# Grouped attention: the value product with tokens on partitions, division by the softmax sums behind it

## The chip, the cores and the metric

The kernel runs on one core of one Trainium2 chip. The metric is the device time of one execution in microseconds (us); the median over several executions is compared. The engines are named as in the profile: PE (TensorE, matrix products; PEld are its weight loads), DVE (VectorE), ACT (ScalarE), POOL (GpSimd) and SP (SyncE, which issues transfers).

## The reference, cut to what matters

The model is two layers of a hybrid block: a state-space branch, grouped attention, differential attention and a gated recurrence, merged, and then a feed-forward part. 256 latent tokens and 256 context tokens run through it; the second layer gives out the latent tokens alone. The change touches grouped attention only: 8 query heads of 64 features, two key and value heads.

```python
def gqa_core(q, k, v):
    s = jnp.einsum('bqgrd,bkgd->bgrqk', q, k) * ATTN_SCALE
    p = softmax32(s).astype(v.dtype)
    return jnp.einsum('bgrqk,bkgd->bqgrd', p, v)
```

## The kernel before

Activations lie with features on partitions and tokens along the free axis. Layer 0 has four tiles of 128 tokens (two latent ones, which attend to all 512 keys, and two context ones, which attend to 256); layer 1 has the two latent tiles. Dense products are made in three float32r matmuls of high and low parts (`mm3`, lines 267 to 269), into four PSUM accumulators of the pool `big`. Attention uses four others, of the pool `small`.

Grouped attention is made in two halves of four heads (`gqa_half`). Its queries come from `q_half`: for each token tile a dense product into a `big` tile, then the norm and the rotation (`rope_of`: a product with the cosines into `fo`, L611, one with the sines into `fth`, L617, and their sum, L619), four transposes (`twice`, L625) and the split into high and low parts. The accumulator is free only when L611 and L617 have read it. The name `fth` stands for two buffers, which tiles take in turn in program order.

For each token tile and head, `soft` makes the scores of 512 or 256 keys (two matmuls, L731 and L732), the row maximum (L734, DVE), the exponential with its sum (L737, ACT), the reciprocal of the sum (L762) and the scaled exponentials (L763, both DVE). Two steps later, `value` transposes the probabilities in blocks of 128 keys (`pT`: L589 on PE, the copy L742 on ACT) and, once both heads of a pair are there, multiplies them with the values (L777): V is the stationary side with 64 columns, the transposed probabilities move with 128 columns, and the two heads write partitions 0 to 63 and 64 to 127 of the output. After two pairs a copy (L780, DVE) puts the tile into the half's output, which has features on partitions already.

`staged` runs the stages with a lag of two steps and gives their instructions high priority; `along` puts merge products of another branch (L1076 on: a dense product with 512 or 256 columns into `big`) between them in program order. The order on the engines is then set by the scheduler of the framework, which plays the program through with its own times and picks what is ready; so a change in one loop can move instructions elsewhere.

Of the kernel before, what the change touches and what calls it, by code (L numbers as in the profile page):

```python
# [9 lines left out]
F32 = mybir.dt.float32  # L10
# [4 lines left out]
OP = mybir.AluOpType  # L15
# [192 lines left out]
def _build(ctx, nc, tc, I, out, dbg):  # L208
    PSUM = bass.MemoryType.PSUM

    def pool(name, bufs, **kw):
        return ctx.enter_context(tc.tile_pool(name=name, bufs=bufs, **kw))
# [9 lines left out]
    sp = pool("sp", 4)  # L222
# [3 lines left out]
    V, S, G, PE = nc.vector, nc.scalar, nc.gpsimd, nc.tensor  # L226
# [5 lines left out]
    def small(n=512):  # L232
        p = pm.tile([128, 512], F32, name="small")
        return p[:, :n]

    def tt(name, n=512, dt=F32, bufs=None):

        x = tmp.tile([128, 512], dt, name=name, bufs=bufs or 3)
        return x[:, :n]
# [4 lines left out]
    def blk(ap, d):  # L244
        return ap.rearrange("p (h d) -> p h d", d=d)

    def bc(ap, shape):
        return ap.to_broadcast(shape)
# [306 lines left out]
    class Mixer:  # L555
# [198 lines left out]
                yield  # L754

        def gqa_half(self, i, qs, o):
            ets, ops = {}, {}

            def soft(c, _):
                t, pr, half = c  # L760
                e, s, k0, kn = self.probs(qs[t], self.gk, 2 * pr + half, half, t)
                V.reciprocal(s, s)  # L762
                V.tensor_scalar(e, e, s, None, op0=OP.mult)  # L763
                return e, k0, kn

            def value(c, x):
                t, pr, half = c
                e, k0, kn = x
                ets[half] = self.pT(e, kn)
                if not half:  # L770
                    return
                if not pr:
                    ops[t] = small(256)
                for kb in range(kn):
                    for z in range(2):
                        hs = slice(z * 64, z * 64 + 64)
                        PE.matmul(ops[t][hs, pr * 128:(pr + 1) * 128], self.gv[:, k0 + kb, hs],  # L777
                                  ets[z][:, kb * 128:(kb + 1) * 128], start=kb == 0, stop=kb == kn - 1)
                if pr:
                    V.tensor_copy(o[:, :, t * 128:(t + 1) * 128], blk(ops.pop(t), 128))  # L780

            return self.staged([(t, pr, z) for t in range(self.nt) for pr in range(2) for z in range(2)],
                               [soft, value], 2)

        def diff_half(self, i, qs, kT, v, o):
            p, n = self.p, self.n
# [407 lines left out]
    def place(c, ps):  # L1194

        row = ap_.tile([2, 512], F32, name="row", bufs=2)
        V.tensor_copy(row, ps[0:2])
        tp = small(8)
        for i in range(4):
            PE.transpose(tp[:, i * 2:i * 2 + 2], row[:, i * 128:(i + 1) * 128], ident[0:2, 0:2])  # L1200
        i0 = c % 2 * 8 + c // 2 * 4
        V.tensor_copy(mods[0][:, i0:i0 + 4], tp.rearrange("p (i v) -> p i v", v=2))

    before = None
    for c in range(4):

        ps = small()
        for k in range(0, KT, 2):
            z = c * 4 + k // 2
# [17 lines left out]
    for l in range(DEPTH):  # L1227
# [44 lines left out]
        qs = mx.q_half("gq", 0, 0)  # L1272
# [8 lines left out]
        qs = mx.q_half("gq", 0, 1)  # L1281
# [6 lines left out]
        qs = mx.q_half("dq", 2, 0)  # L1288
# [5 lines left out]
        qs = mx.q_half("dq", 2, 1)  # L1294
# [46 lines left out]
```

## Time and profile before

| what | value |
|---|---|
| median of 3 runs | 1808.97 us |
| the profiled execution | 1808.46 us, span 1806.7 us |
| share of the span in which PE is busy | 94% |
| DVE, ACT, POOL | 69%, 51%, 47% |
| mean granted clock of PE | 0.975 of full speed |

The span runs from the first to the last instruction; what is around it, some 1.8 us, is part of the time. PE's clock has two levels, 2.4 GHz (1.00) and 1.2 GHz (0.50); a mean between them is a mixture of both. A PE that is busy isn't at its peak: matmuls overlap, and what one costs is read from one start to the next.

### The profile page before, as it was taken

To read this page: it belongs to the slowest core of one execution; us is meant where nothing else is said; L and a number is where in the kernel's file an instruction comes from. 1 tells how busy PE (TensorE), PEld (TensorE's weight loads), DVE (VectorE), ACT (ScalarE), POOL (GpSimd) and SP (SyncE) were. 2 spreads that over 40 slices of the span, in tenths; PEclk is the share of its full clock that TensorE was granted. 3 is DMA by queue.
4 is the path that set the end of the run, shared out by engine and by line. 5 is a ranking of instruction groups with operands and counts; after the bars stand their busy time and mean duration, and the time that the engine had idled before them with its cause. 6 is when DMAs were issued, how large, how long until landed. Compare 5 with 4: busy or idle time off the path is not lost.

```text
span 1806.7 us, 27888 instructions
## 1 busy us (share of the span) xinstructions
PE 1702.3 (94%) x10734; PEld 1490.2 (82%) x10734; DVE 1243.0 (69%) x2233; ACT 925.0 (51%) x1685; POOL 855.6 (47%) x522
## 2 busy tenths in 40 slices
PE   6979999989989998999999999978999999989999
PEld 1866788878888787987778889866888999989998
DVE  6697757766868676798756465677767667567664
ACT  3635654544544554465544343646555555556554
POOL 4353655342535657566534342454773345433443
PEclk9989999999999999999999999988999999989999
DMA  7221423221323355535655453222243133445553
GB/s 294 87 94 52 139 90 119 89 90 45 105 77 113 98 183 209 187 123 172 201 186 176 136 166 106 87 94 93 95 141 117 48 118 120 172 150 184 187 184 127
DMA packets 52037, 237.10 MB, mean 131 GB/s; under 512 B 9664, under 2 KB 12608, under 8 KB 34496
## 3 DMA queue, kind: packets, MB, share of 16 engines
q1 hardware_dynamic: 28080, 179.46, 28.7%
q10 hardware_dynamic: 23824, 55.86, 9.7%
q8 instruction: 85, 1.39, 0.3%
q14 instruction: 48, 0.39, 0.1%
HBM read 234.18 MB, written 1.11 MB: 130 GB/s over the span
## 4 chain that ended last, share of the span: by engine, by line
PE 39%; DVE 5%; DMA 2%; POOL 2%; ACT 2%; issue 1%; ACTq 0%; POOLq 0%; DVEq 0%; SPq 0%
PE big L267 12%; PE big L268 12%; PE big L269 12%; DMA w<-in_w 1%; POOL whl L251 1%; DMA wa<-in_w 1%; POOL wa L431 1%; PE small L777 1%; ACT whl L256 1%; PE small L589 1%; DVE whl L251 1%; PE small L625 0%; DVE fo L552 0%; PE small L731 0%; DVE B L1033 0%
## 5 line engine op out<-in xcount | busy, mean ns | idle before, releaser
L251 POOL TENSOR_TENSOR whl<-w,whl 128x1024 fp32r<-128x1024 f32 (+3 forms) x194 | 450.6, 2326 | 528.0 <-ACT whl L256 490.2
L267 PE MATMUL big<-hh,whl 128*128 128x256 f32 (+1 forms) x1632 | 549.0, 341 | 24.6 <-ACT sq L668 9.1
L268 PE MATMUL big<-hl,whl 128*128 128x256 f32 (+1 forms) x1632 | 549.5, 338 | 0.8 <-POOL hl L251 0.8
L269 PE MATMUL big<-hh,whl 128*128 128x256 f32 (+1 forms) x1632 | 549.6, 338 | 0.0
L256 ACT CAST whl<-w 128x1024 fp32r<-128x1024 f32 (+3 forms) x342 | 334.6, 985 | 171.3 <-PE big L269 81.9
L267 PEld LDWEIGHTS big<-hh,whl 128*128 128x128 f32 x1632 | 312.2, 193 | 61.0 <-issue 15.7
L268 PEld LDWEIGHTS big<-hl,whl 128*128 128x128 f32 x1632 | 314.3, 193 | 33.3 <-issue 3.4
L269 PEld LDWEIGHTS big<-hh,whl 128*128 128x128 f32 x1632 | 314.4, 193 | 33.2 <-issue 3.4
L251 DVE TENSOR_TENSOR whl<-w,whl 128x1024 fp32r<-128x1024 f32 (+2 forms) x150 | 198.7, 1326 | 68.1 <-ACT whl L256 67.7
L552 DVE SCALAR_TENSOR_TENSOR fo<-big,pp,fo 128x510 f32<-128x510 f32 (+2 forms) x224 | 141.0, 633 | 79.4 <-ACT fo L544 75.8
L431 POOL TENSOR_TENSOR wa<-wa,crow 128x1024 f32<-128x1024 f32 x48 | 126.9, 2646 | 76.4 <-DVE fo L435 44.8
L267 PE MATMUL big<-whl,hl 128*128 128x256 f32 (+1 forms) x512 | 148.9, 292 | 3.5 <-DVE sq L1044 3.0
L268 PE MATMUL big<-whl,hh 128*128 128x256 f32 (+1 forms) x512 | 149.7, 293 | 2.0 <-POOL whl L251 2.0
L269 PE MATMUL big<-whl,hh 128*128 128x256 f32 (+1 forms) x512 | 149.4, 292 | 0.0
L267 PE MATMUL big<-act,whl 128*128 128x256 f32 (+1 forms) x392 | 125.4, 320 | 4.1 <-POOL whl L251 4.1
L269 PE MATMUL big<-act,whl 128*128 128x256 f32 (+1 forms) x392 | 125.6, 321 | 0.0
L268 PE MATMUL big<-act,whl 128*128 128x256 f32 (+1 forms) x392 | 125.4, 320 | 0.0
L544 ACT ACTIVATE fo<-big,pp 128x512 f32<-128x512 f32 (+1 forms) x104 | 71.0, 683 | 97.4 <-PE big L269 89.6
L267 PEld LDWEIGHTS big<-whl,hl 128*128 128x128 f32 x512 | 100.1, 196 | 5.3 <-DVE sq L1044 3.2
L268 PEld LDWEIGHTS big<-whl,hh 128*128 128x128 f32 x512 | 100.5, 196 | 3.7 <-POOL whl L251 2.2
L269 PEld LDWEIGHTS big<-whl,hh 128*128 128x128 f32 x512 | 100.4, 196 | 1.2 <-issue 1.0
L267 PE MATMUL big<-bo,whl 128*128 128x512 f32 (+1 forms) x256 | 89.1, 349 | 9.7 <-POOL whl L251 9.3
(296 smaller groups left out, 3265.3 us busy)
## 6 DMA issues: line engine op xcount, KB each, us to landing
w<-in_w SPq DMA_DIRECT2D x136, 1024.0 KB, 4.9
wa<-in_w ACTq DMA_DIRECT2D x64, 512.0 KB, 3.6
w<-in_w SPq DMA_DIRECT2D x16, 768.0 KB, 4.3
w<-in_w SPq DMA_DIRECT2D x16, 640.0 KB, 3.9
bcm<-in_w ACTq DMA_DIRECT2D x14, 512.0 KB, 3.6
q<-csd ACTq DMA_DIRECT2D x24, 256.0 KB, 4.3
wa<-in_w SPq DMA_DIRECT2D x11, 512.0 KB, 8.5
xm<-in_xT ACTq DMA_DIRECT2D x8, 512.0 KB, 7.5
```

Of the source, the lines that this page charges most:

```text
L251: eng.tensor_tensor(o, v, hi.bitcast(F32), op=OP.subtract)
L256: S.copy(m.h, v)
L267: PE.matmul(ps, a.l, b.h, start=start, stop=False)
L268: PE.matmul(ps, a.h, b.l, start=False, stop=False)
L269: PE.matmul(ps, a.h, b.h, start=False, stop=stop)
L431: G.tensor_tensor(w, w, cr, op=OP.mult)
L544: S.activation(o, ps, AF.Identity, scale=wt[:, nc_ + c:nc_ + c + 1], bias=b[:, c:c + 1])
L552: V.scalar_tensor_tensor(os_, is_, wt[:, j * nc_ + c:j * nc_ + c + 1], os_, op0=OP.mult, op1=OP.add)
L589: PE.transpose(ps[:, i * 128:(i + 1) * 128], s, ident)
L777: PE.matmul(ops[t][hs, pr * 128:(pr + 1) * 128], self.gv[:, k0 + kb, hs], ets[z][:, kb * 128:(kb + 1) * 128], start=kb == 0, stop=kb == kn ...
```

## The change

Each head is now a step of its own in `value`. The transposed probabilities are the stationary side (128 columns), V moves with 64 columns, and the output has tokens on partitions and the four heads of the half side by side along the free axis. The exponentials aren't scaled; the reciprocals of a tile's four sums are kept in `rs4`, and one DVE product per token tile (L780 in the changed kernel) multiplies the four heads' outputs with them on the way out of PSUM, into a buffer of the name `fth`. A third stage, `place`, two steps later, transposes that tile in two blocks (PE, L589 through `transposes`) and copies it into the half's output (ACT, L787).

```diff
             def soft(c, _):
-                t, pr, half = c
-                e, s, k0, kn = self.probs(qs[t], self.gk, 2 * pr + half, half, t)
-                V.reciprocal(s, s)
-                V.tensor_scalar(e, e, s, None, op0=OP.mult)
+                t, hd = c
+                e, s, k0, kn = self.probs(qs[t], self.gk, hd, hd % 2, t)
+                if not hd:
+                    rs[t] = sp.tile([128, 4], F32, name="rs4", bufs=2)
+                V.reciprocal(rs[t][:, hd:hd + 1], s)
                 return e, k0, kn
 
             def value(c, x):
-                t, pr, half = c
+                t, hd = c
                 e, k0, kn = x
-                ets[half] = self.pT(e, kn)
-                if not half:
+                et = self.pT(e, kn)
+                if not hd:
+                    ops[t] = small(256)
+                vs = slice(hd % 2 * 64, hd % 2 * 64 + 64)
+                for kb in range(kn):
+                    PE.matmul(ops[t][:, hd * 64:(hd + 1) * 64], et[:, kb * 128:(kb + 1) * 128],
+                              self.gv[:, k0 + kb, vs], start=kb == 0, stop=kb == kn - 1)
+                if hd < 3:
                     return
-                if not pr:
-                    ops[t] = small(256)
-                for kb in range(kn):
-                    for z in range(2):
-                        hs = slice(z * 64, z * 64 + 64)
-                        PE.matmul(ops[t][hs, pr * 128:(pr + 1) * 128], self.gv[:, k0 + kb, hs],
-                                  ets[z][:, kb * 128:(kb + 1) * 128], start=kb == 0, stop=kb == kn - 1)
-                if pr:
-                    V.tensor_copy(o[:, :, t * 128:(t + 1) * 128], blk(ops.pop(t), 128))
+                f = tt("fth", 256, bufs=2)
+                V.tensor_tensor(blk(f, 64), blk(ops.pop(t), 64), bc(rs.pop(t)[:, :, None], [128, 4, 64]), op=OP.mult)
+                return f
+
+            def place(c, f):
+                t, hd = c
+                if hd == 3:
+                    self.transposes([f[:, 0:128], f[:, 128:256]],
+                                    lambda q: S.copy(o[:, :, t * 128:(t + 1) * 128], q))
```

The order of the instructions moves with it. On DVE, in the first half of layer 0's grouped attention, the rotation of the second half's first query tile (L611, L617, tile `tab`) stood between the early heads before. The names are `sm` the sums, `e` the exponentials, `tab` the table of sines and cosines.

```order
L762 RECIPROCAL sm<-sm 128x1
L611 TENSOR_TENSOR fo<-big,tab_2500 128x256
L617 TENSOR_TENSOR fth<-big,tab_2500 128x256
L302 TENSOR_SCALAR xs<-xs 128x512
L635 TENSOR_SCALAR ss<-ss 128x4
L763 TENSOR_SCALAR e<-e,sm 128x512
```

In the changed kernel L611 of that tile stands at about the same place, but L617 comes only behind the product L780 of the half's last token tile, on the same engine:

```order
L734 TENSOR_REDUCE mx<-small 128x1
L780 TENSOR_TENSOR fth<-small,rs_2907 128x256
L764 RECIPROCAL rs_2987<-sm 128x1
L734 TENSOR_REDUCE mx<-small 128x1
L764 RECIPROCAL rs_2987<-sm 128x1
L780 TENSOR_TENSOR fth<-small,rs_2987 128x256
L617 TENSOR_TENSOR fth<-big,tab_2500 128x256
L619 TENSOR_TENSOR fo<-fo,fth 128x256
```

L617 has moved from the fourth head's place to behind the sixteenth's.

On PE, in the same half, at the heads of the context tiles, merge products of 512 columns (L267 to L269) stood between one head's matmuls and the next before:

```order
L267 MATMUL big<-hh,whl 128x512
L268 MATMUL big<-hl,whl 128x512
L589 MATMUL small<-cst,e 128x128 x3
L731 MATMUL small<-kp,q 128x256
L732 MATMUL small<-kp,q 128x256
L589 MATMUL small<-cst,e 128x128 x3
L777 MATMUL small<-et,gv 64x128
L269 MATMUL big<-hh,whl 128x512
```

The same heads in the changed kernel, where L775 is the value product:

```order
L775 MATMUL small<-gv,et 128x64 x4
L589 MATMUL small<-cst,e 128x128 x4
L731 MATMUL small<-kp,q 128x256
L732 MATMUL small<-kp,q 128x256
L589 MATMUL small<-cst,e 128x128 x4
L731 MATMUL small<-kp,q 128x256
L732 MATMUL small<-kp,q 128x256
L775 MATMUL small<-gv,et 128x64 x4
L589 MATMUL small<-cst,e 128x128 x2
L775 MATMUL small<-gv,et 128x64 x5
```

The merge products have moved behind the half's last transposes; from the last head of 512 keys on, attention stands alone on PE until then.

## Rows read from the trace of the kernel before

**Rows 1.** The page's part 1: busy us, share of the span, instructions.

```profile
PE 1702.3 (94%) x10734; PEld 1490.2 (82%) x10734; DVE 1243.0 (69%) x2233; ACT 925.0 (51%) x1685; POOL 855.6 (47%) x522
```

**Rows 2.** Windows: stretch, us, each engine's busy us, clock, DMA share, GB/s.

```profile
350.00:396.00 46.00, 46.00 (x297) 38.95 (x295) 25.20 (x47) 20.77 (x45) 16.63 (x8) 1.00 0.26 85
396.00:403.40 7.40, 2.13 (x12) 1.25 (x11) 7.40 (x9) 2.65 (x7) 4.84 (x2) 0.84 0.11 44
403.40:410.20 6.80, 6.40 (x46) 4.88 (x45) 5.87 (x12) 4.67 (x11) 2.36 (x1) 0.67 0.66 231
1400.00:1450.00 50.00, 50.00 (x404) 45.61 (x405) 34.01 (x74) 25.49 (x48) 17.68 (x11) 1.00 0.17 57
```

**Rows 3.** Timeline of PE, layer 0: start us, us, engine, line, names, shapes, records.

```profile
324.04 0.28 PE L267 MATMUL big<-whl,hl 128*128 128x256 f32 x1
324.16 0.28 PE L268 MATMUL big<-whl,hh 128*128 128x256 f32 x1
324.37 0.43 PE L777 MATMUL small<-et,gv 128*64 128x128 f32 x2
324.73 0.50 PE L731 MATMUL small<-kp,q 128*128 128x512 f32 x1
325.07 0.39 PE L732 MATMUL small<-kp,q 128*128 128x512 f32 x1
325.30 0.28 PE L269 MATMUL big<-whl,hh 128*128 128x256 f32 x1
...
328.11 0.40 PE L732 MATMUL small<-kp,q 128*128 128x512 f32 x1
328.43 1.09 PE L777 MATMUL small<-et,gv 128*64 128x128 f32 x14
329.45 0.39 PE L269 MATMUL big<-whl,hh 128*128 128x256 f32 x1
329.67 0.28 PE L267 MATMUL big<-whl,hl 128*128 128x256 f32 x1
```

**Rows 4.** Timeline of PE, layer 1: the last block of value products.

```profile
1429.95 1.09 PE L777 MATMUL small<-et,gv 128*64 128x128 f32 x14
```

**Rows 5.** Timeline of PE in `ssd_decay`: 32 and 64 columns over 128 stationary.

```profile
157.90 0.39 PE L846 MATMUL small<-da,cst 128*128 128x32 f32 x2
158.13 0.41 PE L847 MATMUL small<-da,ones 128*128 128x64 f32 x2
158.35 0.47 PE L267 MATMUL big<-hh,whl 128*128 128x512 f32 x1
```

**Rows 6.** Groups by line, DVE: busy us, mean ns, idle us before.

```profile
L763 DVE TENSOR_SCALAR e<-e,sm 128x512 f32<-128x512 f32 (+1 forms) x48 | 30.4, 637 | 1.2
```

**Rows 7.** Timeline of all engines around the gap; in brackets idle before, and releaser.

```profile
396.45 5.14 DVE L763 TENSOR_SCALAR e<-e,sm 128x512 f32<-128x512 f32 x2
396.47 2.34 POOL L431 TENSOR_TENSOR bcm<-bcm,xs 128x1024 f32<-128x1024 f32 x1 [3.88 <-DVE sm L762]
398.78 2.53 POOL L251 TENSOR_TENSOR whl<-w,whl 128x1024 fp32r<-128x1024 f32 x1
399.24 0.63 PE L589 MATMUL small<-cst,e 128*128 128x128 f32 x4 [3.10 <-DVE e L763]
...
402.23 0.69 ACT L737 ACTIVATE e<-small,mx 128x512 f32<-128x512 f32 x1 [4.75 <-DVE mx L734]
...
403.06 1.12 PE L589 MATMUL small<-cst,e 128*128 128x128 f32 x4 [2.16 <-ACT e L737]
```

**Rows 8.** Groups by line and shape, 311 to 445 us: heads of 256 keys.

```profile
L737 ACT ACTIVATE e<-small,mx 128x256 f32<-128x256 f32 x16 | 7.7, 483 | 11.2 <-DVE mx L734 11.2
L734 DVE TENSOR_REDUCE mx<-small 128x1 f32<-128x256 f32 x16 | 6.7, 421 | 12.3 <-PE small L732 12.2
L742 ACT COPY et<-small 128x256 f32<-128x256 f32 x16 | 5.9, 372 | 7.7 <-PE small L589 4.2 <-PE small L777 3.4
```

**Rows 9.** Timeline of DVE: a split of branch 0 beside GpSimd.

```profile
318.28 2.35 DVE L251 TENSOR_TENSOR bo<-xs,bo 128x512 fp32r<-128x512 f32 x1
```

More of the change, by code (lines that the diff above doesn't have):

```diff
@@ L756, in gqa_half @@
         def gqa_half(self, i, qs, o):
-            ets, ops = {}, {}
+            ops, rs = {}, {}
             def soft(c, _):
-                t, pr, half = c
-                e, s, k0, kn = self.probs(qs[t], self.gk, 2 * pr + half, half, t)
-                V.reciprocal(s, s)
-                V.tensor_scalar(e, e, s, None, op0=OP.mult)
+                t, hd = c
[3 more added lines that the diff above has]
+                V.reciprocal(rs[t][:, hd:hd + 1], s)
@@ L779, in value @@
-                if pr:
-                    V.tensor_copy(o[:, :, t * 128:(t + 1) * 128], blk(ops.pop(t), 128))
-            return self.staged([(t, pr, z) for t in range(self.nt) for pr in range(2) for z in range(2)],
-                               [soft, value], 2)
+                et = self.pT(e, kn)
[5 more added lines that the diff above has]
+                              self.gv[:, k0 + kb, vs], start=kb == 0, stop=kb == kn - 1)
@@ new lines, in value @@
+                if hd < 3:
+                    return
+                f = tt("fth", 256, bufs=2)
[6 more added lines that the diff above has]
+                                    lambda q: S.copy(o[:, :, t * 128:(t + 1) * 128], q))
+            return self.staged([(t, hd) for t in range(self.nt) for hd in range(4)], [soft, value, place], 2)
```

## The prediction

> **What bounds the kernel now.** I read the busy times of the page first, then TensorE's (PE's) share in the stretches where grouped attention runs. PE is busy for 1702 of 1807 us, VectorE (DVE), the next one, for 1243 [rows 1]. So a microsecond leaves the run only if it leaves PE's own work or a gap in PE. The loop that the diff rewrites, `gqa_half`, runs from about 311 to 445 us (layer 0, 32 pairs of a head and a token tile) and from 1369 to 1431 us (layer 1, 16). Nearly everywhere in it PE is full: 46.0 of the 46 us up to 396 us, 50.0 of the 50 from 1400 us [rows 2]. Work taken from DVE under that cover is worth nothing by itself; only PE's own instructions count there. One hole lies in the loop: from 396.0 to 403.4 us PE is busy for 2.1 of 7.4 us, and in the 6.8 us after that the mean granted clock is 0.67, so PE runs at 1.2 GHz for a part of them [rows 2]. These two things, PE's own cost and that hole, carry the sum.
>
> **PE's value products.** Before, a value matmul has 64 stationary columns (V) and 128 moving ones; the two heads of a pair write the two halves of the output's partitions. Each float32 matmul is two records in the trace. What a block of them costs is read from one dense neighbour's start to another's [rows 3]: a matmul of 256 columns takes 0.12 us from start to start (324.04 to 324.16), one of 512 columns 0.23 (325.07 to 325.30). A block of 2 records: 324.16 to 325.07 is 0.91 us, less 0.12 and 0.23 for the dense matmul on either side, is 0.56 us. A block of 14: 328.11 to 329.67 is 1.56, less 0.23 and 0.12, is 1.21 us. Twelve records more cost 0.65 us, so two records, one of each head, cost 0.11 together: the two heads overlap fully. What is left is 0.45 us for each block, whatever its length: the entry into that half-array form and the way out. The timeline has 57 blocks, the first at 324.37 us and the last at 1429.95 [rows 3, 4]. So the 320 records cost 160 x 0.11 + 57 x 0.45 = 17.6 + 25.7 = 43.3 us of PE.
>
> After, the transposed probabilities are stationary (128 columns) and V moves with 64 columns, one head at a time: 160 matmuls again, 320 records, in the whole array, with nothing to enter. That form is in the trace of before: the sums of `ssd_decay` move 32 and 64 columns over 128 stationary ones, and four such records move the next start from 157.90 to 158.35 us, 0.112 each [rows 5]. I take 320 x 0.112 = 35.8 us. The bounds are 0.055, half of a pair today, and 0.112; the rows of the very form stand at the upper end. New are 24 transposes of the finished tiles, 48 records, 5.4 us at the same price. On PE that makes 35.8 + 5.4 - 43.3 = -2.1 us.
>
> The Trainium skill, "TensorEngine Tiling (Array Packing)", section "When to Use Tiling", speaks against this edit: for a moving side of 64 columns or fewer it advises to swap the operands and tile the columns in two, which is the form given up here. By that rule alone PE would go from 17.6 to 41.2 us. The 0.45 us of each block is what the rule leaves out; the same page, "Key Properties", says that a change of tiling mode drains the engine, and the trace agrees.
>
> **DVE and ScalarE (ACT).** The 48 scalings of the exponentials go, 30.4 us of DVE, 0.64 in the mean [rows 6]. The 48 reciprocals stay. The 12 copies of the output become 12 products over the same 128x256 elements; I cost the difference at nothing, since PE's full rows cover both, and with that cover gone it would be a few tenths each. ACT gets 12 copies of 256 columns, 0.37 us each by the copies of transposed probabilities [rows 8]: 4.5 us on an engine that is half idle. This matters only where PE starves.
>
> **The hole.** At 396.45 us DVE begins two scalings that take 5.14 us together, in the time in which GpSimd runs two long products (396.47 to 401.31) [rows 7]. PE's transposes wait 3.10 us for the first. The next row maximum is queued behind the second on DVE, its exponential on ACT waits 4.75 us for that, and PE another 2.16 us for the exponential [rows 7]. Gaps: 5.3 us. The clock of 0.67 over 6.8 us in which PE is nearly always busy takes (1 - 0.67) x 6.8 = 2.2 us [rows 2]. Together 7.5 us. After, the transposes read the exponentials straight from ACT, and no scaling stands ahead of a maximum, so I take all 7.5 off. The bounds are 0 and 7.5, since GpSimd's long products stay and other DVE instructions can meet them; that is a rival.
>
> **The new wait.** The finished tile goes into the `fth` buffers, of which there are two, and `rope_of` of the next queries uses the same two. In program order the first two query tiles of the second half get the buffers of the last finished tiles of the first half. The order shows what follows: the rope product L617 of the first query tile stood right behind its partner L611; now it stands behind the last finished tile of the half. Queued behind it on DVE are the rest of that rope and the next tile's. Until it is done, the four query tiles hold all four `big` accumulators, and the merge matmuls of 512 columns, which were spread over the first half, can't start. So PE gets a bare run of attention. By the order, in it are 32 value matmuls (7.2 us at 0.224), 28 transposes of probabilities (6.3), 9 pairs of score matmuls, one with 512 keys (0.46) and 8 with 256 (0.24 each), and 8 transposes of finished tiles (1.8): 17.7 us. Is PE fed in it? ACT has 24 instructions of 0.37 to 0.69 us in it and 9 short readings of sums, some 12 us; DVE has less [rows 7, 8]. In the order a head's transposes come about two heads behind its scores. From scores to exponential it takes some 1.4 us (0.3 to reach DVE, 0.42 maximum, 0.48 exponential, hand-overs), and the heads between cover that. Stepping through the order by hand with these lengths, I find two waits of 0.2 us for a copy and one of 0.8 us at the end, where the last finished tile and then the rope product must pass DVE: 1.2 us. ACT's queue adds to it; I take 3 us. The bounds are 0 and no overlap at all, where a head of 256 keys takes 2.8 us (0.24 + 0.3 + 0.42 + 0.48 + 0.22 + 0.3 + 0.37 + 0.45) in place of 1.0 and one of 512, at 1.6 times that, 4.4 in place of 1.8: 8 x 1.8 + 3 x 2.6 = 22 us. With two heads in flight the rows are near the lower end.
>
> In the second half of layer 0 and in layer 1 the new order leaves dense work between most heads, and layer 1's stretch has no gap today, so there only PE's own sum counts.
>
> **The sum.** The profiled execution took 1808.46 us for a span of 1806.7, and the median shown is 1808.97, so a change of the span goes straight to the median: 1809 - 2.1 - 7.5 + 3 = 1802.4, taken as 1802 us. The scheduler also moves some work of the second layer's recurrence, ahead of its attention; with no row that gives it a sign I allow it 3 us either way. With the other small uncertainties the forecast's own range is 1797 to 1807.
>
> **Rivals.** The hole returns in other clothes: GpSimd's long products still run near the start of the second half, and a DVE instruction of 512 columns that is no scaling took 2.35 us at 318.28 us [rows 9]. For it: those products keep their place in the order. Against it: dense merges now stand between the heads there. Then only PE's own sum is left: 1809 - 2.1 = 1807.
>
> The new wait is dear, and the kernel slower than before: the bare run costs what two heads in flight fail to hide, and the clock falls behind it as it did at 403 us. It decides when it costs more than 9.6 us (2.1 + 7.5). Midway between that and the serial bound of 22 us, 16 us give 1809 - 9.6 + 16 = 1815. For it: 17.7 us without a dense matmul in the order. Against it: the steps above.
>
> The overlap of the two heads was the whole matter: PE pays 41.2 in place of 17.6 us and gets nothing back: 1809 + 23.6 - 7.5 + 3 = 1828. The 0.45 us of each block speaks against it. This is the tiling rule of the Trainium skill taken as it stands.
>
> Narrow matmuls are cheap: at 0.055 us a record PE saves another 18 us: 1784. The rows at 157.90 us speak against it.
>
> **How the numbers follow.** Forecast 0.55 (1802), hole returns 0.17 (1807), dear wait 0.20 (1815), overlap lost 0.03 (1828), cheap records 0.05 (1784). From 1795 to 1813 the range leaves out the cheap records, the lost overlap and half of the dear wait, 0.18. Two per cent, about what a measurement of this kernel can tell from no change, is 36 us, and no case reaches it: within 2% has 0.96, and 0.02 stand on each side for a schedule that goes another way altogether.
>
> **What would show it.** Value records 0.112 us apart, with no step of 0.2 us on the way in or out; no gap of over 1 us on PE where the second half begins, and a clock of 1.00 there; PE busy for over 85% of the bare run, at whose end L617 waits for the last finished tile. I am wrong if that run has a gap of some microsecond for each head, if the clock falls in it, or if the gaps of layer 1's recurrence grow by more than all this.

## The result, and the profile after

The changed kernel takes 1795.59 us in the median of 4 runs (1793.39 to 1797.61). The kernel before took 1808.51, 1808.97 and 1812.11 us beside it; a fourth run of it, at 1877.34 us, was in a slower state of the chip and is left out. The ratio is 0.993, with a 95% interval of 0.9916 to 0.9944. On the median that the prediction started from, this is a gain of 12.7 us, where 6.6 were forecast. The time lies just inside the range of 1795 to 1813, and outside the 1797 to 1807 that I gave the forecast itself; nothing here is near 2%, as I had expected. The point was missed by half of the effect, and the experiments below show that the gain has another cause than the one I gave.

The profiled execution took 1793.39 us for a span of 1791.6. The page's first part (busy us, share, instructions) answers to [rows 1]:

```profile
PE 1698.7 (95%) x10758; PEld 1502.5 (84%) x10758; DVE 1231.9 (69%) x2185; ACT 928.2 (52%) x1697; POOL 860.1 (48%) x522
```

The span is 15.1 us shorter, and PE is busy for 3.6 us less. So most of the gain is idle time of PE. DVE lost 48 scalings, 30.4 us before [rows 6], but its busy time fell by 11.1 only, so what the rest of its instructions take has grown by some 19.

The windows of [rows 2] again, then two more, 334 to 351 and 375 to 381 us:

```profile
350.00:396.00 46.00, 45.48 (x239) 38.01 (x238) 29.65 (x50) 22.54 (x42) 23.77 (x12) 1.00 0.31 104
396.00:403.40 7.40, 7.40 (x65) 7.31 (x64) 1.95 (x7) 3.71 (x11) 3.62 (x2) 1.00 0.35 122
403.40:410.20 6.80, 6.80 (x62) 6.80 (x61) 1.60 (x5) 2.66 (x8) 0.00 (x0) 1.00 0.06 24
1400.00:1450.00 50.00, 50.00 (x413) 49.25 (x412) 37.74 (x76) 26.99 (x54) 21.36 (x15) 1.00 0.32 106
334.00:351.00 17.00, 15.28 (x120) 13.35 (x118) 7.67 (x25) 11.30 (x34) 3.33 (x2) 1.00 0.01 1
375.00:381.00 6.00, 6.00 (x34) 5.08 (x33) 6.00 (x7) 1.04 (x2) 4.93 (x2) 1.00 0.61 222
```

The hole is gone: 7.40 of 7.40 us where 2.13 were busy, at a clock of 1.00. The bare run of attention is there, 15.28 of 17 us. Its largest gaps, and what ends it, in the timelines of PE and of DVE:

```profile
344.02 0.44 PE L589 MATMUL small<-cst,e 128*128 128x128 f32 x2 [0.33 <-ACT e L737]
346.30 0.43 PE L775 MATMUL small<-gv,et 128*128 128x64 f32 x2 [0.51 <-ACT et L742]
350.71 0.44 PE L589 MATMUL small<-cst,fth 128*128 128x128 f32 x2 [0.52 <-DVE fth L780]
351.04 0.50 PE L267 MATMUL big<-hh,whl 128*128 128x512 f32 x1
...
350.23 0.43 DVE L780 TENSOR_TENSOR fth<-small,rs 128x256 f32<-128x256 f32 x1 [1.51 <-PE small L775]
350.57 0.41 DVE L617 TENSOR_TENSOR fth<-big,tab 128x256 f32<-128x256 f32 x1
```

As predicted, L617 follows the half's last finished tile, and the merges (L267, 512 columns) start then. The value products, in PE's timeline, answer to [rows 3]:

```profile
329.56 0.40 PE L732 MATMUL small<-kp,q 128*128 128x512 f32 x1
329.79 1.00 PE L775 MATMUL small<-gv,et 128*128 128x64 f32 x8
330.60 0.36 PE L268 MATMUL big<-whl,hh 128*128 128x256 f32 x1
330.80 0.28 PE L269 MATMUL big<-whl,hh 128*128 128x256 f32 x1
```

Eight records and one dense matmul take 1.01 us from start to start (329.79 to 330.80); less the dense one's 0.12 that is 0.89, or 0.111 a record. There is no step of 0.45 us. A straight line through all blocks at the full clock that have no idle time beside them says the same of both traces: 0.050 us a record and 0.45 a block before (56 of 57 blocks), 0.111 a record and nothing a block after (65 of 67).

Where the 15.1 us left, by landmarks on PE (start in us, from the timelines; the last two columns are two of the kernels below):

| landmark | before | changed | shared buffers alone | layer 0 alone |
|---|---|---|---|---|
| layer 0, first grouped scores | 311.1 | 310.5 | 310.4 | 310.8 |
| layer 0, first differential scores | 463.3 | 456.2 | 455.2 | 456.5 |
| first product with the merged branches (`mm`) | 707.2 | 699.4 | 691.4 | 699.6 |
| layer 1, decay sums (fifth `da,cst`) | 1240.9 | 1231.7 | 1226.2 | 1232.2 |
| layer 1, first grouped scores | 1358.2 | 1339.6 | 1343.4 | 1340.1 |
| layer 1, first differential scores | 1448.6 | 1435.9 | 1432.9 | 1436.7 |
| last product of the feed-forward part (`act`) | 1801.5 | 1786.4 | 1785.7 | 1789.4 |

Layer 0's grouped attention gave 6.5 us (463.3 - 311.1 less 456.2 - 310.5). From layer 1's decay sums to its differential scores 3.5 more left: the recurrence became 9.4 shorter and the grouped attention behind it 5.9 longer, since work of PE moved from the one into the other (770 and 708 matmul records before, 698 and 797 after). The rest is spread in pieces of 0.6 to 2.4 us.

### The profile page after: what moved, and what is told of

It is laid out like the page before. It is cut to its first block, busy times and chain, and to the rows that moved or that the text cites. A ratio compares the mean times of both kernels' runs of the same rounds, so it can differ in the third digit from the quotient of the medians.

```text
span 1791.6 us, 27916 instructions
## 1 busy us (share of the span) xinstructions
PE 1698.7 (95%) x10758; PEld 1502.5 (84%) x10758; DVE 1231.9 (69%) x2185; ACT 928.2 (52%) x1697; POOL 860.1 (48%) x522
## 4 chain that ended last, share of the span: by engine, by line
PE 46%; DVE 6%; ACT 3%; DMA 2%; POOL 2%; issue 2%; ACTq 0%; POOLq 0%; DVEq 0%; SPq 0%
PE big L267 14%; PE big L268 14%; PE big L269 14%; DMA w<-in_w 1%; POOL whl L251 1%; DVE fo L435 1%; DMA wa<-in_w 1%; DVE whl L251 1%; PE small L589 1%; PE small L775 1%; DVE fo L552 1%; ACT whl L256 1%; PE small L625 0%; PE small L731 0%; PE small L732 0%
## 5 line engine op out<-in xcount | busy, mean ns | idle before, releaser
L251 POOL TENSOR_TENSOR whl<-w,whl 128x1024 fp32r<-128x1024 f32 (+3 forms) x194 | 455.4, 2350 | 534.2 <-ACT whl L256 502.0
L267 PE MATMUL big<-hh,whl 128*128 128x256 f32 (+1 forms) x1632 | 550.8, 342 | 25.2 <-ACT sq L668 9.1
L269 PE MATMUL big<-hh,whl 128*128 128x256 f32 (+1 forms) x1632 | 552.1, 340 | 0.0
L267 PEld LDWEIGHTS big<-hh,whl 128*128 128x128 f32 x1632 | 314.4, 195 | 61.2 <-issue 12.6
L269 PEld LDWEIGHTS big<-hh,whl 128*128 128x128 f32 x1632 | 316.1, 194 | 32.9 <-issue 2.8
L251 DVE TENSOR_TENSOR whl<-w,whl 128x1024 fp32r<-128x1024 f32 (+2 forms) x150 | 204.2, 1363 | 55.3 <-ACT whl L256 53.1
L267 PE MATMUL big<-whl,hl 128*128 128x256 f32 (+1 forms) x512 | 147.0, 289 | 3.5 <-DVE sq L1050 3.0
L268 PE MATMUL big<-whl,hh 128*128 128x256 f32 (+1 forms) x512 | 147.9, 289 | 2.3 <-POOL whl L251 2.3
L269 PE MATMUL big<-whl,hh 128*128 128x256 f32 (+1 forms) x512 | 147.5, 289 | 0.0
L267 PE MATMUL big<-act,whl 128*128 128x256 f32 (+1 forms) x392 | 125.1, 319 | 0.2 <-POOL whl L251 0.2
L269 PE MATMUL big<-act,whl 128*128 128x256 f32 (+1 forms) x392 | 124.9, 319 | 0.0
L267 PEld LDWEIGHTS big<-whl,hl 128*128 128x128 f32 x512 | 98.2, 193 | 4.3 <-DVE sq L1050 3.2
L269 PEld LDWEIGHTS big<-whl,hh 128*128 128x128 f32 x512 | 98.7, 193 | 0.0
L267 PE MATMUL big<-bo,whl 128*128 128x512 f32 (+1 forms) x256 | 88.5, 348 | 6.5 <-POOL whl L251 4.0
```

The source lines that it names most:

```text
L251: eng.tensor_tensor(o, v, hi.bitcast(F32), op=OP.subtract)
L267: PE.matmul(ps, a.l, b.h, start=start, stop=False)
L268: PE.matmul(ps, a.h, b.l, start=False, stop=False)
L269: PE.matmul(ps, a.h, b.h, start=False, stop=stop)
```

## The experiments

The theory at first was the prediction's: the scalings on DVE made the hole, and taking them away closed it. The rivals: the form of the value product; and the new order, which comes from sharing the `fth` buffers.

**Without the scalings** (the form of before; the division is left out).

```diff
                 V.reciprocal(s, s)
-                V.tensor_scalar(e, e, s, None, op0=OP.mult)
```

> The kernel before without the scaling of the exponentials (the division is left out altogether, the reciprocals stay). Theory A, the scalings made the gap at 396 to 410 us: that gap is gone and the time falls by some 7.5 us against before, PE's value blocks still cost some 43 us. Rival B, the gain comes from the form of the value products and from other moves of the order: no more than 2 us fall here.

Measured: 1802.87 us, 0.9975 (0.9963 to 0.9986), 4.5 us faster than the 1807.38 beside it, between the two expectations. In its trace layer 0's grouped attention is 6.4 us shorter, and the window from 385 to 412 us, which holds the hole in the kernel before, is nearly full (first the kernel before, then this one):

```profile
385.00:412.00 27.00, 21.34 (x151) 17.74 (x149) 23.30 (x40) 15.57 (x34) 12.89 (x5) 0.87 0.37 130
385.00:412.00 27.00, 25.97 (x205) 22.98 (x204) 17.12 (x32) 17.37 (x39) 15.77 (x8) 1.00 0.39 129
```

So the hole can be closed this way, in that stretch at about the price that I gave it. That doesn't yet say that the changed kernel closed it this way.

**The changed kernel with the scalings kept.**

```diff
-                V.reciprocal(rs[t][:, hd:hd + 1], s)
+                V.reciprocal(s, s)
+                V.tensor_scalar(e, e, s, None, op0=OP.mult)
...
-                V.tensor_tensor(blk(f, 64), blk(ops.pop(t), 64), bc(rs.pop(t)[:, :, None], [128, 4, 64]), op=OP.mult)
+                V.tensor_copy(f, ops.pop(t))
```

> The changed kernel with the exponentials scaled by DVE as before and a plain copy on the way out of PSUM. Theory A: only PE's own sum is left of the gain and the wait on the shared buffers stays, so it stands between 2 us below and 6 us above before. Rival B: most of the 13 us measured are kept, 8 us or more below before.

Measured: 1809.76 us, 1.0017 (1.0004 to 1.003), 3.1 us slower than before and inside theory A's range. The hole did not stay where it was: 385 to 412 us is full but for 0.5 us. The bare run is the dear place now. At its start the copy that PE waits for (L742) stands on ACT behind a cast of weights and an exponential, with no merge to put into the gap, and the window behind that has a clock of half (timelines of ACT and PE, window):

```profile
333.46 1.04 ACT L256 CAST whl<-w 128x1024 fp32r<-128x1024 f32 x1
334.40 0.70 ACT L737 ACTIVATE e<-small,mx 128x512 f32<-128x512 f32 x1
...
335.07 0.59 ACT L742 COPY et<-small 128x512 f32<-128x512 f32 x1
...
335.72 0.69 PE L774 MATMUL small<-gv,et 128*128 128x64 f32 x2 [1.71 <-ACT et L742]
...
335.20:355.70 20.50, 19.61 (x89) 18.51 (x90) 9.24 (x25) 8.72 (x27) 2.88 (x2) 0.50 0.01 2
```

At half the clock 19.6 busy us hold 9.8 us of work at the full one. This is the rival "the new wait is dear", clock and all. Without the scalings the bare run of this form stays cheap. How the scalings bring this about isn't shown: none of PE's waits in layer 0's grouped attention is put down to one, and the execution profiled, at 1814.40 us, is the second slowest of the twelve.

**The changed kernel with the finished tile in a buffer of its own.** (Its room comes from a small tile of the recurrence, `csr`, which has one buffer in place of two.)

```diff
-                f = tt("fth", 256, bufs=2)
+                f = tmp.tile([128, 256], F32, name="gm", bufs=1)
...
-            csr = tmp.tile([128, 128], F32, name="gm", bufs=2)[0:64]
+            csr = tmp.tile([128, 256], F32, name="gm", bufs=1)[0:64, 0:128]
```

> The changed kernel with the finished tile in a buffer of its own (one buffer, shared with a tile used only in the decay step) instead of the two that the rotation uses. Theory A: dense merge products come back into the first half's bare run and the time falls by some 3 us against the changed kernel. Rival C: the bare run costs PE nothing, or the run only moves to another place; within 2 us of the changed kernel.

Measured: 1811.59 us, 1.0025 (1.0014 to 1.0037): 4.5 us slower than before by the ratio, and so some 17 us slower than the changed kernel. Both theories had it within 3 us of the changed kernel; both are wrong here. The merges are back between the heads of the first half, which is full; the second half starts bare, and the hole is back in it, in a kernel whose exponentials aren't scaled (timelines of DVE and PE, then a window and that of 385 to 412):

```profile
395.17 2.50 DVE L251 TENSOR_TENSOR whl<-w,whl 128x1024 fp32r<-128x1024 f32 x1
...
399.14 0.66 PE L589 MATMUL small<-cst,e 128*128 128x128 f32 x4 [3.04 <-ACT e L737]
402.26 0.69 PE L775 MATMUL small<-gv,et 128*128 128x64 f32 x2 [2.46 <-ACT et L742]
...
399.90:406.70 6.80, 4.44 (x16) 3.67 (x16) 4.54 (x7) 3.18 (x6) 4.65 (x2) 0.50 0.67 220
385.00:412.00 27.00, 20.37 (x141) 18.08 (x139) 19.01 (x34) 15.62 (x33) 13.61 (x5) 0.87 0.39 133
```

Another DVE instruction, a split of weights, now stands ahead of the row maxima, which start at 397.60 us; the second wait is for a copy that stands behind two exponentials and an activation of weights on ACT. The scaling was only what happened to stand there before.

**128 stationary columns in the form of before**, with the scalings: each head multiplies both heads' values in the whole array, and two copies cut out the halves that count.

```diff
-                    ops[t] = small(256)
+                    ops[t] = small(512)
...
-                        PE.matmul(ops[t][hs, pr * 128:(pr + 1) * 128], self.gv[:, k0 + kb, hs],
+                        PE.matmul(ops[t][:, (2 * pr + z) * 128:(2 * pr + z + 1) * 128], self.gv[:, k0 + kb],
```

> The kernel before (scaled exponentials, features on partitions) with 128 stationary columns of V for each head, of which the copy takes the right 64 partitions (two copies of half the partitions instead of one): no half-array form and no overlap of two heads. Theory A, 0.45 us for each block are paid for entering and leaving the half-array form: value products cost 320 x 0.112 = 36 us of PE instead of 43, and the time falls by some 5 to 8 us. The rule of tiling taken alone: PE pays 18 us more, the time rises by 10 us or more.

Measured: 1801.78 us, 0.9977 (0.9964 to 0.9991), 4.2 us faster, a little less than theory A's price, and no loss. The Trainium skill, "TensorEngine Tiling (Array Packing)", section "When to Use Tiling", advises to tile the columns in two where the stationary side has 64; this run goes the other way, as the 0.45 us of each block has it [rows 3]. But part of the gain is the hole's, and this run can't tell how much. The hole is all but gone (1.8 of 27 us idle, at a clock of 1.00) although the scalings are there, one of them stretched to 2.43 us (timeline of DVE, window):

```profile
392.05 2.43 DVE L763 TENSOR_SCALAR e<-e,sm 128x512 f32<-128x512 f32 x1
...
385.00:412.00 27.00, 25.17 (x203) 24.03 (x201) 22.78 (x45) 17.13 (x40) 13.75 (x7) 1.00 0.41 137
```

A scaling is thus neither needed for the hole nor enough for it. The new theory: what matters is where PE has no merge products left to put beside a stretched DVE instruction, and the shared buffers decide that.

**The shared buffers alone:** before, scalings and half-array form and all, with the output led through a `fth` tile.

```diff
-                    V.tensor_copy(o[:, :, t * 128:(t + 1) * 128], blk(ops.pop(t), 128))
+                    f = tt("fth", 256, bufs=2)
+                    V.tensor_copy(f, ops.pop(t))
+                    S.copy(o[:, :, t * 128:(t + 1) * 128], blk(f, 128))
```

> The kernel before, with its scalings and its half-array value products, but the finished tile goes out through one of the two fth buffers (12 copies of 256 columns more, on ACT). The order shows that the 512-column merges leave the first half for the second, just as in the changed kernel. Theory A (the shared buffers are good only when the scalings are gone; with them the bare run becomes the hole, as in the kernel with the scalings kept): about 5 us slower than before (the 3.1 of that kernel and the 2.1 of PE's own work that it saved), with the half clock in the bare run around 335 to 360 us and no hole at 396. Theory B (the buffers are good by themselves): 4 us or more faster than before.

Measured: 1793.92 us, 0.9935 (0.9919 to 0.995). Theory B: with the old value product and the scalings, and only the shared buffer and one more copy on ACT, this kernel has the changed kernel's time. The stretched scaling is still there; PE has merges there, and waits 0.32 us for the scaling before it and not at all for this one (timeline of DVE, windows):

```profile
381.00 2.62 DVE L763 TENSOR_SCALAR e<-e,sm 128x512 f32<-128x512 f32 x1
...
385.00:412.00 27.00, 27.00 (x204) 22.87 (x202) 12.06 (x29) 13.42 (x35) 5.79 (x4) 1.00 0.23 79
335.00:355.00 20.00, 17.42 (x124) 12.74 (x125) 13.84 (x39) 9.74 (x33) 4.06 (x5) 1.00 0.01 2
```

The bare run costs 2.6 us here, without a fall of the clock, though the scalings are in it; theory A, drawn from the second experiment, was wrong.

This gain doesn't lie in grouped attention alone. By the landmarks 7.5 us left there, and 7.6 between the first differential scores of layer 0 and the first merged product, where PE has nearly the same records. There it waits less and keeps its full clock (windows, the kernel before and then this one):

```profile
463.00:707.00 244.00, 229.12 (x1220) 196.64 (x1219) 177.53 (x287) 120.92 (x254) 137.04 (x74) 0.97 0.38 126
463.00:707.00 244.00, 230.29 (x1287) 198.08 (x1286) 181.27 (x289) 123.77 (x256) 144.88 (x76) 1.00 0.40 136
```

No run here shows why.

**The change in one layer alone** (the changed function in one layer, that of before in the other), and the changed kernel on the same chip.

```diff
         def gqa_half(self, i, qs, o):
+            if self.full:
+                return self.gqa_new(i, qs, o)
```

For layer 1 the condition is `not self.full`.

> The change in layer 0's grouped attention alone, layer 1 as before. Theory A (the gain is layer 0's attention, where half a dozen us left in the trace, and the rest of the difference between the two traces is from elsewhere): 7 to 9 us faster than before, and the changed kernel in the same call no more than 2 us better. Theory B (the 3.5 us that the second layer's recurrence and attention gained in the trace belong to the change there): this kernel stays 3 to 5 us behind the changed one.

> The change in layer 1's grouped attention alone. By PE's own work (a third of the pairs, the transposes of 4 finished tiles) it is worth 1 us (theory A). Theory B: 3 to 5 us faster than before, with the step from the recurrence's start to the end of the attention shorter by as much.

> The changed kernel itself on the chip of the other three, in more runs. Theory A and theory B alike: 0.993 of before, some 12 to 13 us faster; what the other three are worth is read against it.

Measured: layer 0 alone 1797.72 us, 0.9951 (0.9937 to 0.9965), 8.9 us faster than its 1807.0; layer 1 alone 1805.58, 0.9993 (0.9982 to 1.0004); the changed kernel 1794.36, 0.9933 (0.9919 to 0.9946). Most of the gain is layer 0's, as theory A has it. But some 3 us are left between this kernel and the changed one, which theory A put at no more than 2 and theory B at 3 to 5; the two intervals overlap, so these runs don't decide that. Layer 1 alone is PE's own sum, some 1 us, or nothing. The landmarks show one thing more: with layer 1's code as before, layer 1's recurrence is shorter by 9.4 us and the attention behind it longer by 6.2. So the order there was moved by layer 0's edit.

**Shared buffers without scalings; shared buffers with 128 stationary columns.** The edits are those above, put together.

> The kernel before with the finished tile through the fth buffers and without the scalings (the division is left out). Theory A (with the merges kept for the second half, the scalings stand under full rows of PE and cost nothing, as the prediction costs them): within 3 us of the kernel with the buffers alone, so 9 to 15 us faster than before. Theory B (scalings and buffers gain separately, 4.5 and 12 us): 15 us or more faster than before.

> The kernel before with the finished tile through the fth buffers, and with 128 stationary columns in the value products in place of the half-array form (scalings kept, the output cut out of the larger result by two copies). By the price of the half-array form alone (0.45 us for each block, less the longer records: the 4 us that it gave without the buffers) 4 us more than the buffers: 16 us faster than before (theory A). Theory B (what falls in the bare run of the first half decides: shorter matmul rows there leave PE waiting for scalings, as in the kernel with the scalings kept): no better than the buffers alone, or worse.

Measured: 1791.78 us, 0.9926 (0.9905 to 0.9947), and 1800.08 us, 0.9968 (0.9954 to 0.9982), both beside 1806.72. The scalings are worth nothing that shows on top of the buffers (0.9926 and 0.9935, with intervals that overlap): theory A. Leaving the half-array form, which went with a gain of 4 us beside the direct copy, is worth less than nothing here: 5.8 us faster than before where the buffers alone gave 11.7, as theory B has it. By the page PE is busy for 0.8 us less (1694.4 in place of 1695.2) and idle for 5.8 us more (1795.8 - 1694.4 in place of 1790.8 - 1695.2). Little of that lies in the bare run, the place that theory B named: from 335 to 355 us PE is busy for 17.19 us, and with the buffers alone for 17.42. A gap of 1.44 us opened at 382.31, and the rest is in small pieces, so the cause stays open.

**The merges held back, without sharing buffers.** In the kernel before, the merge products that go along with the second half of layer 0's grouped attention are ordered on PE behind the first half's last value product; then the same in the changed kernel with its own buffer.

```diff
+                    with tc.issue_after(mark) if mark else nullcontext():
                         mx.merge(b, bm, m, [js.pop(0)], first=first, fill=fill)
```

> The kernel before, with its scalings, its half-array form and its direct copy out; only the merge products that go along with the second half of layer 0's grouped attention are ordered on PE behind the last value product of the first half. No buffer is shared. The order on PE is then nearly that of the kernel with the buffers alone. Theory A (the shared buffers gain because they hold the merges back): 8 to 14 us faster than before. Theory B (they gain by something else, such as the later rotations or the copies that moved to ACT): no more than 4 us faster.

> The changed kernel with the finished tile in a buffer of its own, as in the run that lost the gain, and the merge products of the second half ordered behind the last value product of the first. Theory A (the place of the merges is all that the own buffer took away): 0.992 to 0.996 of before, near the changed kernel. Theory B: it stays near 1.0025.

Measured: before with merges held 1804.59 us, 0.9983 (0.9972 to 0.9994); the own buffer with merges held 1796.07 us, 0.9939 (0.992 to 0.9957). The second is theory A's: holding the merges gives back what the own buffer took, and the bare run is as in the changed kernel. The first, some 3 us faster, lies in theory B's range. Its second half is full, as theory A has it, but part of the gain is lost again in the bare run (timelines, then windows):

```profile
336.14 2.33 POOL L251 TENSOR_TENSOR whl<-w,whl 128x1024 fp32r<-128x1024 f32 x1
336.26 2.76 DVE L643 TENSOR_TENSOR fo<-fo,r 128x512 f32<-128x512 f32 x1
339.56 0.63 PE L589 MATMUL small<-cst,e 128*128 128x128 f32 x4 [4.07 <-DVE sm L762]
...
385.00:412.00 27.00, 27.00 (x189) 22.38 (x188) 10.82 (x24) 11.79 (x26) 7.33 (x4) 1.00 0.21 79
339.50:346.40 6.90, 6.84 (x48) 5.53 (x50) 3.83 (x13) 3.36 (x9) 1.20 (x1) 0.75 0.00 0
```

L643 belongs to the next half's queries. With the shared buffers it waits behind the finished tiles, out of the bare run (351.54 us in the changed kernel, 0.69 us long); here it stands in it, meets GpSimd, and the scaling behind it comes 2.76 us later. So the shared buffers do two things, hold the merges and hold the rotations; in the kernel with scalings the first alone is not enough. That the second is what is missing is read from this trace and not tested: no run holds the rotations alone, or leads the old form's tile through a buffer of its own. And it is the smaller part: of the 12.4 us by which this trace is longer than that of the shared buffers alone (spans of 1803.2 and 1790.8), 3.4 lie in layer 0's grouped attention and 7.3 in the stretch behind it, up to the first merged product.

The ratios side by side:

| | direct copy or own buffer | shared `fth` | merges held |
|---|---|---|---|
| form of before, scaled | 1 | 0.9935 | 0.9983 |
| form of before, not scaled | 0.9975 | 0.9926 | |
| 128 stationary columns, scaled | 0.9977 | 0.9968 | |
| changed form, not scaled | 1.0025 | 0.993, 0.9933 | 0.9939 |
| changed form, scaled | | 1.0017 | |

No version is faster than the changed kernel by more than the intervals allow.

## Why the prediction was half right

**PE's value products: right.** 0.111 a record where 0.112 was taken, no entry step, and layer 1 alone at 0.9993 agrees with a third of -2.1 us. That PE's sum goes straight to the time doesn't hold everywhere: with the shared buffers and 128 stationary columns PE was idle for more than the form saved.

**DVE and ACT: right at the place that the sum spoke of.** With the merges in place the scalings are worth nothing that shows (0.9926 beside 0.9935). In the changed form, though, the kernel with scalings (1.0017) and the one without (0.9933) lie 15 us apart, for which the sum had no term. A part is the clock: its mean is 0.975 over the 12 runs of the one and 0.978 over the 6 of the other, and one less this mean, times the span, gives 45 and 39 us, an estimate of 6 of the 15. What makes the rest is open.

**The hole: its size right, its cause wrong.** Taking only the scalings away shortens layer 0's grouped attention by 6.4 us, near my 7.5. But "no scaling stands ahead of a maximum, so I take all 7.5 off" was a wrong step: without scalings and with its own buffer the hole is back at 399 us, behind a split of weights, as the rival of other clothes said. In the changed kernel the hole is closed because merges stand there; the run with its own buffer and the merges held back shows it (0.9939). One of the longest DVE instructions of the whole stretch falls into its second half, and PE doesn't notice (timelines of POOL and DVE; the window 375 to 381 above has 6.00 of 6.00 us):

```profile
376.56 3.37 POOL L431 TENSOR_TENSOR bcm<-bcm,xs 128x1024 f32<-128x1024 f32 x1
...
377.68 3.33 DVE L435 SCALAR_TENSOR_TENSOR fo<-A,xs 128x1024 bf16<-128x1024 f32 x1
```

**The new wait: this is the step that failed.** Its own price was about right: 1.7 us of idle in the bare run (17 less 15.28), 3 forecast. What I left out is what it buys. I wrote that in the second half "the new order leaves dense work between most heads", used it as an argument against a rival, and gave it no number; the merges held back by the shared buffers are that dense work. Between the changed kernel and the same one with its own buffer lie 17 us (1.0025 and 0.9933 of some 1807); in the kernel before, the sharing alone is worth some 12. By the landmarks 10.4 of the 17 us lie in layer 0's grouped attention (156.1 us there with its own buffer, 145.7 in the changed kernel), and the rest of the change costs 3.9 there (156.1 beside the 152.2 of before). So the term of +3 should have been one of some -10, with the hole's 7.5 in it and not beside it: the two are not to be added.

For that stretch the sum came out near all the same: two thirds of PE's 2.1, with the 7.5 and less the 3, is 5.9 us, and 6.5 left. That was luck, since the price belonged to another cause. The rest of the trace's 15.1 us left where the sum had only the 3 us either way: 3.5 from layer 1's decay sums to its differential scores, and 5 in small pieces, which no run here explains.

**Layer 1's recurrence: 3 us allowed, 3.5 found in the trace,** and of either sign. Three kernels besides the changed one show the same shift (layer 0 alone, the scalings kept, and merges held in the kernel before), the shared buffers alone don't; they gain 7.6 us between the first differential scores of layer 0 and the first merged product instead, where the changed kernel gains 0.7. So the two equal times are made up of different pieces, and why the one or the other comes about is open.

**The rivals.** The hole returned only with the own buffer, the dear wait only with the scalings kept. The lost overlap and the cheap records are refuted by the records above. All the signs that I had named came true: the records' 0.111 us, no gap of 1 us where the second half begins and a clock of 1.00 there, 90% of the bare run busy, L617 behind the last finished tile. But none of them could tell a hole that is closed because the scalings are gone from one that is filled with merges.

## What to carry to other kernels

Look at every buffer name that an edit newly shares: what waits for the buffer moves, and here that moved more than the arithmetic did. A gap is made by two things, a stretched step of the chain and the lack of other work beside it; ask for both, and where independent work is saved up by a delay, count the place to which it goes as well as the one that it leaves. Terms of a sum that name the same gap are one term; test the side effect alone, with the rest of the edit undone. And name signs that the rival would not give as well.

## What was not expected of the hardware

Some DVE instructions that meet a long GpSimd product take about the rest of that product more. L643 takes 0.69 us alone, and 2.76 where it began 0.12 us into a GpSimd product of 2.33: it ended 0.55 us after it (336.26 + 2.76 against 336.14 + 2.33). L435 ended 1.08 us after its GpSimd product (377.68 + 3.33 against 376.56 + 3.37), and takes 1.21 alone (at 362.60 in the same kernel). The Trainium skill, "SBUF — State Buffer", section "SBUF: two separate sides", calls the pair of ports that the two engines share an exclusive lock for the whole instruction; these rows agree. Not every DVE instruction is stretched: the row maxima L734, which read PSUM, take 0.67 to 0.69 us for 512 columns in the kernel before, both the 26 that begin while a GpSimd instruction of over 2 us runs and the 38 that don't.

The clock did not fall after each gap. In the kernel with the scalings kept it is 0.50 for 20.5 us beside a gap of 1.71 us; with the shared buffers alone a gap of 1.42 us at 336.74, at about the same place, leaves it at 1.00. Nothing here tells these two apart. Over all their runs the mean clock is 0.975 and 0.9775, so the 20.5 us are not a measure of what the clock costs between the two kernels: by the estimate above that is some 5 us of the 15.
